# A two-layer hybrid encoder: ten of the sixteen gate tiles of each mixer's last two merges made in pairs by seven block products

## The chip, the cores and the metric

The kernel runs on one core of a Trainium2 chip, as one program that is launched once. The metric is the device time of that program in microseconds (us), the median of several executions. All data is f32; products are made on the matrix engine (TensorE, "PE" in the profile) from values split into a rounded high part and a low rest (`fp32r`). The other engines named here are VectorE (DVE), ScalarE (ACT), GpSimd (POOL) and the queue from which almost all transfers are issued (SP).

## The reference

Two layers work on x (512 tokens by 1024 features). Each is a half-step feed-forward net (FFN), a mixer, and a second FFN. What the change touches is the end of the mixer:

```python
proj = h @ w_in                                   # h: 512 x 1024
qa, ka, va, ub, qc, kc, vc, f_lin, g_lin = split(proj)
ya = chunked_relpos_attention(qa, ka, va)         # branch A
yb = multiscale_pool(ub)                          # branch B
yc = forgetting_attention(qc, kc, vc, f_lin)      # branch C
branch = einsum('bsnw,nwd->bsnd', [ya, yb, yc], w_branch)
gates = sigmoid(g_lin.reshape(B, S, 3, 1024))     # g_lin: 512 x 3072
merged = sum over the three branches of gates * branch
x = x + gate2 * (merged @ w_out)
```

So each branch needs a gate of 1024 features, a product of h with a 1024 x 1024 block of weights, and a product of its own output (512 wide) with 512 x 1024 weights.

## The kernel before

**Products.** Everything is kept transposed: features on the 128 partitions, the 512 tokens along the row. A weight chunk of 512 KB is loaded into a `raw` buffer (two exist), ACT casts it to the high part `whi`, DVE subtracts to get the low part `wlo` (three buffers each; `wchunk`, lines 262 to 280). `triple` (line 117) then issues three matmuls for each block of 128 features (high by high, high by low, low by high), each with 512 columns. The normed input h of a stage stands in `hhi` and `hlo`.

**A gate tile** (128 features of a gate for 512 tokens) is 8 such blocks, so 24 matmuls into one PSUM bank. The branch product of the same features is 4 blocks, 12 matmuls. `merge_units(l, n, ys, put)` (line 1053) walks the 8 tiles d of branch n: a chunk of `w_branch` for every second d, the gate's chunk, the gate's matmuls, a tanh on ACT, the branch's matmuls, and `put`, which multiplies the two (DVE), adds to the running sum `m` (POOL), and for the last branch splits the sum into high and low part (`put_b`, line 1138; in `v2` buffers for d below 4, else in `b` buffers).

**Order in the mixer** (`Mixer.run`): attention A, then attention C, with the merge of branch A filled in between its steps. Then the pooled branch's four `pool_front` (line 1010), each with a matmul group, sums over trailing windows on POOL, and a split of the result into a `ptb` buffer. Each is followed 60 units later by its `pool_back` (a unit is one matmul of 512 columns in the program's own count). In between run the merge of branch C (n = 2) and then that of branch B (n = 1). The product with `w_out` (`k_outer`) ends the mixer.

**The FFN's pairs.** In two of its three parts each FFN already makes two gate tiles together. `seven` (line 520) takes the two tiles' weights as a 2 x 2 block matrix (rows: the two tiles; columns: features 0 to 511 and 512 to 1023). The input is a 2 x 2 block matrix too (features by tokens, halves of each). It forms seven products of blocks in place of eight, each 4 blocks of 3 matmuls of 256 columns (`add_product`, lines 128 to 130). For that it needs sums of weight blocks (`tens`, line 529, into `v2`), split into `ptb` (two buffers), and sums of blocks of h, made ahead by `t_tasks` (lines 475 to 499) in `v2` or in place and split into eight `b` buffers. Partial results are copied (ACT) and added (DVE, 256 columns) in a `v2` buffer.

**Queues.** Each engine executes its instructions in the order of its queue. The order is set when the program is built: work is placed by program order and by when a planner expects its inputs. `later(delay, fn)` puts work off until the program's count of matmuls has advanced by `delay`; `poll` issues what is due. A buffer is given to a new tile when its last reader is done. There are 17 `b`, 4 `v2`, 4 `xv`, 3 `whi` and `wlo`, 2 `raw`, 2 `ptb` and 2 `t1` buffers in SBUF, and 4 `acc` and 4 `mm` banks in PSUM.

Of the kernel before, what the change touches and what calls it, by code (L numbers as in the profile page):

```python
# [15 lines left out]
F32 = mybir.dt.float32  # L16
F32R = mybir.dt.float32r
# [23 lines left out]
def encoder_kernel(tc, xT, c, w_ada, b_ada, gains, w_gate, w_up, w_down, w_qkv, w_f, w_ubg,  # L41
# [404 lines left out]

    class Ffn:
# [19 lines left out]

        def t_tasks(self):  # L470

            norm, bias = self.norm, modc[:, self.l, 3 * self.ms]
            self.tforms = [None] * 4
            first, second = slice(0, HALF), slice(HALF, T)
            sub = lambda o, a, b: nc.vector.tensor_tensor(o, a, b, op=ALU.subtract)
            full = [None] * 4

            def h(q):
                if norm is None:
                    full[q] = blk("v2", F32)  # L480
                    k = slice(2 * q, 2 * q + 2)
                    nc.vector.tensor_tensor(full[q], hhi[:, k, :].bitcast(F32), hlo[:, k, :].bitcast(F32), op=ALU.add)
                else:
                    full[q] = norm.xa[q]
                    for a in range(2):
                        d = 2 * q + a
                        nc.scalar.activation(full[q][:, a, :], full[q][:, a, :], AF.Identity, bias=bias[:, d:d + 1])

            def t1_t3(m):
                b1, b2 = full[m], full[m + 2]  # L490
                sub(b1[:, :, first], b1[:, :, second], b1[:, :, first])
                sub(b1[:, :, second], b2[:, :, second], b1[:, :, second])

            def t2_t4(m):
                b1, b2 = full[m], full[m + 2]
                sub(b2[:, :, second], b2[:, :, second], b1[:, :, first])
                sub(b2[:, :, first], b2[:, :, first], b2[:, :, second])

            def parts(q):
                self.tforms[q] = blk("b"), blk("b")  # L500
                split_to(*self.tforms[q], full[q])

            r = []
            for m in range(2):
                for fn, i in ((h, m), (h, m + 2), (t1_t3, m), (parts, m), (t2_t4, m), (parts, m + 2)):
                    r.append(lambda fn=fn, i=i: fn(i))
            return r

        def rights(self, name):

            first, second = slice(0, HALF), slice(HALF, T)
            if name[0] == "B":
                k0 = 4 * (int(name[1]) - 1)
                cols = (first, second)[int(name[2]) - 1]
                return [(hhi[:, k0 + k, cols], hlo[:, k0 + k, cols]) for k in range(4)]
            q0, cols = {"T1": (0, first), "T3": (0, second), "T4": (2, first), "T2": (2, second)}[name]
            tf = self.tforms
            return [tuple(part[:, k % 2, cols] for part in tf[q0 + k // 2]) for k in range(4)]

        def seven(self, which, n):  # L520

            src = (w_gate, w_up)[which][self.l, self.s]
            raws = []
            for i in range(2):
                side_work()
                raw = st([P, KD, P], F32, "raw", NRAW)
                last["dma"] = nc.sync.dma_start(raw, src[n + i]).ins
                raws.append(raw)
            tens = lambda o, a, b, op: nc.vector.tensor_tensor(o, a, b, op=op)
            a11, a12, a21, a22 = raws[0][:, :4], raws[0][:, 4:], raws[1][:, :4], raws[1][:, 4:]  # L530
            ah, al = st([P, KD, P], F32R, "whi", 3), st([P, KD, P], F32R, "wlo", 3)
            split_to(ah, al, raws[0])
            bh, bl = st([P, 4, P], F32R, "whi", 3), st([P, 4, P], F32R, "wlo", 3)
            split_to(bh, bl, a22)
            s12, s34 = st([P, 2, 4, P], F32, "v2", 4), st([P, 2, 4, P], F32, "v2", 4)
            tens(s12[:, 0], a21, a22, ALU.add)
            tens(s34[:, 0], a11, a21, ALU.subtract)
            tens(s12[:, 1], s12[:, 0], a11, ALU.subtract)
            tens(s34[:, 1], a12, s12[:, 1], ALU.subtract)
            sh, sl = st([P, 4, 4, P], F32R, "ptb", 2), st([P, 4, 4, P], F32R, "ptb", 2)  # L540
            split_to(sh[:, 0:2], sl[:, 0:2], s12)
            split_to(sh[:, 2:4], sl[:, 2:4], s34)
            lefts = {"A11": [(ah[:, k], al[:, k]) for k in range(4)],
                     "A12": [(ah[:, 4 + k], al[:, 4 + k]) for k in range(4)],
                     "A22": [(bh[:, k], bl[:, k]) for k in range(4)]}
            for i, name in enumerate(("S1", "S2", "S3", "S4")):
                lefts[name] = [(sh[:, i, k], sl[:, i, k]) for k in range(4)]
            x, y, w = acc((P, HALF)), acc((P, HALF)), acc((P, HALF))
            c = st([P, 4, HALF], F32, "v2", 4)
            go = lambda o, left, right, start: add_product(o, lefts[left], self.rights(right), start)  # L550
            go(x, "A11", "B11", True)
            nc.scalar.copy(c[:, 0], x)
            go(y, "A12", "B21", True)
            tens(c[:, 0], y, c[:, 0], ALU.add)
            go(x, "S2", "T2", False)
            nc.scalar.copy(c[:, 1], x)
            go(w, "S1", "T1", True)
            nc.scalar.copy(c[:, 2], w)
            go(x, "S3", "T3", False)
            nc.scalar.copy(c[:, 3], x)  # L560
            go(w, "S4", "B22", False)
            tens(c[:, 1], w, c[:, 1], ALU.add)
            tens(c[:, 3], c[:, 2], c[:, 3], ALU.add)
            go(x, "A22", "T4", False)
            return [[c[:, 0:2].rearrange("p a t -> p (a t)")], [x, c[:, 3]]]

        def silu(self, parts):
            sg = t1(T)
            n = T // len(parts)
            for i, p in enumerate(parts):  # L570
                nc.scalar.activation(sg[:, i * n:(i + 1) * n], p, AF.Silu)
            return sg

        def act(self, n, pg, pu, sg=None):
            if sg is None:
                sg = self.silu([pg])
            pr = t2(T)
            nc.vector.tensor_tensor(pr, pu, sg, op=ALU.mult)  # L578
            a = blk("b")
            split_to(a[:, 0, :], a[:, 1, :], pr)  # L580
            return a

        def run(self, nxt):
# [4 lines left out]
            for part, (f0, nf) in enumerate(parts):  # L588
                acts = []
                n = 0  # L590
                if part == 0 and self.norm is None:
                    acts = self.start()
                    n = 3
                    todo = self.t_tasks()
                elif part == 0:
# [18 lines left out]
                    todo = self.t_tasks()  # L614
                if part == 0:
                    for i in range(12):
                        later(T_FIRST + T_STEP * i, lambda i=i: todo.pop(0)() if len(todo) == 12 - i else None)
                elif part == 1:
                    while todo:
                        todo.pop(0)()  # L620
                MOD_RATE[0] = 0.5 if part else 1.0
                while part and n < nf:
                    both = [self.silu(p) for p in self.seven(0, f0 + n)]
# [386 lines left out]
    def pool_front(l, g):  # L1010
# [21 lines left out]
        b = st([P, 2, T], F32R, "ptb", 2)  # L1032
# [20 lines left out]
    def merge_units(l, n, ys, put):  # L1053
        wb = [None]
        gates = {}

        def gate_of(d):
            if d % 2 == 0:
                wb[0] = wchunk(w_branch[l, n, d:d + 2].rearrange("a p k c -> p a k c"), (2, 4, P))
            gh, gl = wchunk(w_ubg[l, 4 + n * KD + d], (KD, P))  # L1060
            pg = gates[d] = acc()
            for k in range(KD):
                triple(pg, gh[:, k, :], gl[:, k, :], hhi[:, k, :], hlo[:, k, :], k == 0, k == KD - 1)
                yield

        for d in range(KD):
# [6 lines left out]
            th = t1(T)  # L1073
            nc.scalar.activation(th, pg, AF.Tanh, scale=0.5)
# [13 lines left out]
    class Mixer:  # L1088
# [10 lines left out]
        def run(self, nxt):  # L1099
# [57 lines left out]
            mc = merge_units(l, 2, yc, put_c)  # L1157
# [5 lines left out]
            mb = merge_units(l, 1, yb, put_b)  # L1163
# [20 lines left out]
    FILL_A, FILL_C = 9.0, 9.0  # L1184

# [66 lines left out]
```

## Time and profile before

| what | value |
|---|---|
| time, median of 3 runs | 2426.74 us (2425.58 to 2429.62) |
| profiled execution | 2427.92 us, its span 2426.2 us |
| ACT busy | 1107.4 us |
| first mixer, pooled branch and last two merges | about 670 to 824 us of the span |
| second mixer, the same | about 1864 to 2024 us of the span |

The profile is of one execution. "Busy" is the time in which an engine had an instruction in work. Matmuls are pipelined, so the duration of one (about 0.39 us at 512 columns) is longer than the spacing from one start to the next. The spacing is what adds up. A page of grouped rows gives line, engine, operation, output and inputs, shape, count, busy us, mean ns of one, and the idle time just before with what ended it.

### The profile page before, as it was taken

How to read it: one execution, taken by the hardware profiler on the slowest of the kernel's cores; microseconds unless marked ns; L12 is line 12 of the kernel's file. 1: busy time of each engine (PE TensorE's matmuls, PEld its weight loads, DVE VectorE, ACT ScalarE, POOL GpSimd, SP SyncE). 2: the span in 40 equal slices, each digit the busy share in tenths (PEclk: the TensorE clock that was granted, in tenths of full speed). 3: DMA queues.
4: the chain of work that ended last, by engine and by line, in shares of the span. 5: the costliest groups of instructions: out<-in, count | busy, mean ns of one | idle time of the engine just before them, and what ended most of it. 6: DMA issues, size and time to landing. Idle time of an engine off the chain costs nothing. (4 is left out here: it accounts for less than half of the span.)

```text
span 2426.2 us, 33833 instructions
## 1 busy us (share of the span) xinstructions
PE 2386.2 (98%) x12954; PEld 2053.5 (85%) x12954; DVE 1555.2 (64%) x2750; ACT 1107.4 (46%) x1898; POOL 343.8 (14%) x423
## 2 busy tenths in 40 slices
PE   7999999999999999999999999999999999999999
PEld 5898988778788898989898989988788888889898
DVE  8977756787543378777468766477866434655463
ACT  5342444786532353424453424466765324534241
POOL 3000011144432210000000000112444222000000
PEclk9999999999999999999999999999999999999999
DMA  7746432223323326464326443323232233222232
GB/s 272 243 156 238 161 137 91 92 79 106 104 87 112 139 104 236 162 228 157 138 80 224 167 150 111 131 70 113 73 116 96 87 122 130 77 97 100 100 105 87
DMA packets 116278, 320.22 MB, mean 132 GB/s; under 512 B 11122, under 2 KB 13298, under 8 KB 116116
## 3 DMA queue, kind: packets, MB, share of 16 engines
q1 hardware_dynamic: 114962, 313.86, 37.5%
q0 software_dynamic: 1152, 4.19, 0.4%
q8 instruction: 102, 1.67, 0.3%
q14 instruction: 60, 0.49, 0.1%
q10 hardware_dynamic: 2, 0.00, 0.0%
HBM read 311.64 MB, written 6.38 MB: 131 GB/s over the span
## 5 line engine op out<-in xcount | busy, mean ns | idle before, releaser
L277 ACT CAST whi<-raw 128x1024 fp32r<-128x1024 f32 (+1 forms) x331 | 344.7, 1045 | 623.4 <-PE acc L120 284.1
L279 DVE TENSOR_TENSOR wlo<-raw,whi 128x1024 fp32r<-128x1024 f32 x323 | 398.2, 1235 | 277.1 <-ACT whi L277 273.3
L119 PE MATMUL acc<-b,whi 128*128 128x512 f32 (+1 forms) x960 | 360.5, 375 | 0.0
L121 PE MATMUL acc<-b,wlo 128*128 128x512 f32 (+1 forms) x960 | 356.7, 372 | 0.3 <-DVE wlo L279 0.3
L120 PE MATMUL acc<-b,whi 128*128 128x512 f32 (+1 forms) x960 | 356.9, 372 | 0.0
L119 PE MATMUL mm<-hhi,whi 128*128 128x512 f32 x792 | 309.1, 391 | 1.4 <-ACT whi L277 1.4
L120 PE MATMUL mm<-hlo,whi 128*128 128x512 f32 x792 | 308.6, 390 | 0.0
L121 PE MATMUL mm<-hhi,wlo 128*128 128x512 f32 x792 | 307.9, 389 | 0.0
L121 PEld LDWEIGHTS acc<-b,wlo 128*128 128x128 f32 x960 | 180.8, 188 | 32.2 <-DVE wlo L279 0.7
L119 PEld LDWEIGHTS acc<-b,whi 128*128 128x128 f32 x960 | 180.8, 188 | 31.5
L120 PEld LDWEIGHTS acc<-b,whi 128*128 128x128 f32 x960 | 180.9, 188 | 30.0
L206 DVE CUSTOM_DVE_ANT_0 v<-v,b,badac 128x1024 f32<-128x1024 f32 x144 | 188.0, 1316 | 20.3 <-DMA v<-in_w_ada_dram 19.9
L119 PE MATMUL acc<-hhi,whi 128*128 128x512 f32 x480 | 191.0, 399 | 3.9 <-ACT whi L277 2.2
L120 PE MATMUL acc<-hlo,whi 128*128 128x512 f32 x480 | 188.1, 392 | 1.1 <-DVE hlo L702 1.1
L121 PE MATMUL acc<-hhi,wlo 128*128 128x512 f32 x480 | 187.4, 391 | 0.0
L119 PEld LDWEIGHTS mm<-hhi,whi 128*128 128x128 f32 x792 | 149.1, 188 | 32.3 <-ACT whi L277 2.3
L121 PEld LDWEIGHTS mm<-hhi,wlo 128*128 128x128 f32 x792 | 148.7, 188 | 31.3
L120 PEld LDWEIGHTS mm<-hlo,whi 128*128 128x128 f32 x792 | 148.8, 188 | 29.3
L578 DVE TENSOR_TENSOR t<-mm,t 128x512 f32<-128x512 f32 x86 | 59.4, 691 | 139.7 <-PE mm L121 138.4
L119 PE MATMUL acc<-whi,hhi 128*128 128x512 f32 x336 | 137.8, 411 | 0.9 <-DVE xv L385 0.9
L121 PE MATMUL acc<-whi,hlo 128*128 128x512 f32 x336 | 132.0, 393 | 0.0
L120 PE MATMUL acc<-wlo,hhi 128*128 128x512 f32 x336 | 131.7, 392 | 0.0
(284 smaller groups left out, 5073.1 us busy)
## 6 DMA issues: line engine op xcount, KB each, us to landing
v<-in_w_ada_dram SPq DMA_DIRECT2D x144, 512.0 KB, 5.2
raw<-in_w_down_dram SPq DMA_DIRECT2D x88, 512.0 KB, 3.3
raw<-in_w_up_dram SPq DMA_DIRECT2D x82, 512.0 KB, 3.2
raw<-in_w_gate_dram SPq DMA_DIRECT2D x79, 512.0 KB, 3.2
raw<-in_w_ubg_dram SPq DMA_DIRECT2D x56, 512.0 KB, 3.2
raw<-in_w_qkv_dram SPq DMA_DIRECT2D x42, 512.0 KB, 3.7
raw<-in_w_branch_dram SPq DMA_DIRECT2D x24, 512.0 KB, 3.6
raw<-in_w_out_dram SPq DMA_DIRECT2D x16, 512.0 KB, 3.2
```

The lines of the kernel that those rows point to most:

```text
L119: mm(o, lh, rh, start=start, stop=False)
L120: mm(o, lh, rl, start=False, stop=False)
L121: mm(o, ll, rh, start=False, stop=stop)
L206: dot = nc.vector.tensor_tensor_reduce(out=raw, in0=raw, in1=silc[0], scale=1.0, scalar=badac[:, l, j, d:d + 1], op0=ALU.mult, op1=ALU.add ...
L277: nc.scalar.copy(hi, raw)
L279: lo_eng.tensor_tensor(lo, raw, hi.bitcast(F32), op=ALU.subtract)
L578: nc.vector.tensor_tensor(pr, pu, sg, op=ALU.mult)
```

## The change

`seven` and the block sums of h move out of the FFN class, unchanged in what they compute there, into a function `seven(srcs, blocks, bank)` and a class `Blocks`. In the mixer a `Blocks` is made after attention C, and its twelve steps are put off to 30, 45, ... 195 units. The merge of branch C makes tiles (4, 5) and (6, 7) by `seven`, that of branch B tiles (0, 1), (2, 3) and (4, 5), with their PSUM in the `mm` banks. The other six tiles stay as they are. In a paired tile the two gate chunks are loaded ahead of the branch chunk; before it was the other way round. `pool_front` splits into a `b` buffer in place of `ptb`; `put_b` always into `b`.

```diff
+    class Blocks:
+        def __init__(self, xa=None, bias=None):
+            self.xa, self.bias = xa, bias
+            self.full, self.parts = [None] * 4, [None] * 4
+            steps = ((self.h, 0), (self.h, 2), (self.t1_t3, 0), (self.split, 0), (self.t2_t4, 0), (self.split, 2))
+            self.todo = [lambda fn=fn, i=i + m: fn(i) for m in range(2) for fn, i in steps]
+        def schedule(self, start, step):
+            count = len(self.todo)
+            for i in range(count):
+                later(start + step * i, lambda i=i: self.todo.pop(0)() if len(self.todo) == count - i else None)
...
+        def h(self, q):
+            if self.xa is None:
+                self.full[q] = blk("v2", F32)
+                k = slice(2 * q, 2 * q + 2)
+                nc.vector.tensor_tensor(self.full[q], hhi[:, k, :].bitcast(F32), hlo[:, k, :].bitcast(F32), op=ALU.add)
...
+        def t1_t3(self, m):
+            b1, b2 = self.full[m], self.full[m + 2]
+            minus(b1[:, :, FIRST], b1[:, :, SECOND], b1[:, :, FIRST])
+            minus(b1[:, :, SECOND], b2[:, :, SECOND], b1[:, :, SECOND])
...
+        def split(self, q):
+            self.parts[q] = blk("b"), blk("b")
+            split_to(*self.parts[q], self.full[q])
...
+    def seven(srcs, blocks, bank):
...
+        ah, al = st([P, KD, P], F32R, "whi", 3), st([P, KD, P], F32R, "wlo", 3)
+        split_to(ah, al, raws[0])
+        bh, bl = st([P, 4, P], F32R, "whi", 3), st([P, 4, P], F32R, "wlo", 3)
+        split_to(bh, bl, a22)
+        s12, s34 = st([P, 2, 4, P], F32, "v2", 4), st([P, 2, 4, P], F32, "v2", 4)
+        tens(s12[:, 0], a21, a22, ALU.add)
+        minus(s34[:, 0], a11, a21)
+        minus(s12[:, 1], s12[:, 0], a11)
+        minus(s34[:, 1], a12, s12[:, 1])
+        sh, sl = st([P, 4, 4, P], F32R, "ptb", 2), st([P, 4, 4, P], F32R, "ptb", 2)
+        split_to(sh[:, 0:2], sl[:, 0:2], s12)
+        split_to(sh[:, 2:4], sl[:, 2:4], s34)
...
+        x, y, w = bank((P, HALF)), bank((P, HALF)), bank((P, HALF))
+        c = st([P, 4, HALF], F32, "v2", 4)
+        go(x, "A11", "B11", True)
+        nc.scalar.copy(c[:, 0], x)
+        go(y, "A12", "B21", True)
+        tens(c[:, 0], y, c[:, 0], ALU.add)
+        go(x, "S2", "T2", False)
+        nc.scalar.copy(c[:, 1], x)
+        go(w, "S1", "T1", True)
+        nc.scalar.copy(c[:, 2], w)
+        go(x, "S3", "T3", False)
+        nc.scalar.copy(c[:, 3], x)
+        go(w, "S4", "B22", False)
+        tens(c[:, 1], w, c[:, 1], ALU.add)
+        tens(c[:, 3], c[:, 2], c[:, 3], ALU.add)
+        go(x, "A22", "T4", False)
+        return [[c[:, 0:2].rearrange("p a t -> p (a t)")], [x, c[:, 3]]]
...
-        b = st([P, 2, T], F32R, "ptb", 2)
+        b = blk("b")
         split_to(b[:, 0, :], b[:, 1, :], df)
...
         def gate_of(d):
+            if d in paired:
+                blocks.finish()
+                both = seven([w_ubg[l, 4 + n * KD + d + i] for i in range(2)], blocks, mmt)
+                for i, p in enumerate(both):
+                    ths[d + i] = apply(p, AF.Tanh, scale=0.5)
+                    gates[d + i] = None
             if d % 2 == 0:
                 wb[0] = wchunk(w_branch[l, n, d:d + 2].rearrange("a p k c -> p a k c"), (2, 4, P))
+            if d in paired:
+                return
             gh, gl = wchunk(w_ubg[l, 4 + n * KD + d], (KD, P))
...
-                b = blk("v2" if d < 4 else "b")
+                b = blk("b")
...
-            mc = merge_units(l, 2, yc, put_c)
+            blocks = Blocks()
+            blocks.schedule(M_FIRST, M_STEP)
+            mc = merge_units(l, 2, yc, put_c, blocks, (4, 6))
...
-            mb = merge_units(l, 1, yb, put_b)
+            mb = merge_units(l, 1, yb, put_b, blocks, (0, 2, 4))
...
+    M_FIRST, M_STEP = 30, 15
```

More of the change, by code (lines that the diff above doesn't have):

```diff
@@ L447, in encoder_kernel, with apply @@
+    def apply(parts, func, **kw):
+        o = t1(T)
+        n = T // len(parts)
+        for i, p in enumerate(parts):
+            nc.scalar.activation(o[:, i * n:(i + 1) * n], p, func, **kw)
+        return o
     class Ffn:
@@ L465, in unit @@
                        k == 0, k == KD - 1)
[L470 to L572, printed above, removed]
         def act(self, n, pg, pu, sg=None):
             if sg is None:
-                sg = self.silu([pg])
+                sg = apply([pg], AF.Silu)
             pr = t2(T)
@@ L613, in run @@
                     n = 2
-                    todo = self.t_tasks()
+                    blocks = Blocks(self.norm.xa, modc[:, l, 3 * ms])
                 if part == 0:
-                    for i in range(12):
-                        later(T_FIRST + T_STEP * i, lambda i=i: todo.pop(0)() if len(todo) == 12 - i else None)
+                    blocks.schedule(T_FIRST, T_STEP)
                 elif part == 1:
-                    while todo:
-                        todo.pop(0)()
+                    blocks.finish()
                 MOD_RATE[0] = 0.5 if part else 1.0
                 while part and n < nf:
-                    both = [self.silu(p) for p in self.seven(0, f0 + n)]
+                    both = [apply(p, AF.Silu)
+                            for p in seven([w_gate[l, s, f0 + n + i] for i in range(2)], blocks, acc)]
                     for i, sg in enumerate(both):
@@ L1050, in wpool_load, with merge_units @@
         return w[:, 0], w[:, 1]
-    def merge_units(l, n, ys, put):
+    def merge_units(l, n, ys, put, blocks=None, paired=()):
         wb = [None]
-        gates = {}
+        gates, ths = {}, {}
         def gate_of(d):
+            if d in paired:
+                blocks.finish()
+                both = seven([w_ubg[l, 4 + n * KD + d + i] for i in range(2)], blocks, mmt)
+                for i, p in enumerate(both):
+                    ths[d + i] = apply(p, AF.Tanh, scale=0.5)
+                    gates[d + i] = None
             if d % 2 == 0:
                 wb[0] = wchunk(w_branch[l, n, d:d + 2].rearrange("a p k c -> p a k c"), (2, 4, P))
+            if d in paired:
+                return
             gh, gl = wchunk(w_ubg[l, 4 + n * KD + d], (KD, P))
@@ L1072, in merge_units @@
             bh, bl = wb[0]
[L1073 to L1074 removed]
+            th = ths[d] if d in ths else apply([pg], AF.Tanh, scale=0.5)
             pb = acc()
@@ L1156, in run @@
             wp = wpool_load(l)
-            mc = merge_units(l, 2, yc, put_c)
+            blocks = Blocks()
+            blocks.schedule(M_FIRST, M_STEP)
+            mc = merge_units(l, 2, yc, put_c, blocks, (4, 6))
             for gi in range(4):
```

37 lines of the change are left out of this document (36 added, 1 removed).

## The prediction

> **What bounds the kernel now.** I read the page's engine table first, then the stretches in which the edited code runs, then the matmuls one by one there and in the FFN, where the same seven products already run.
>
> ```profile
> PE 2386.2 (98%) x12954; PEld 2053.5 (85%) x12954; DVE 1555.2 (64%) x2750; ACT 1107.4 (46%) x1898; POOL 343.8 (14%) x423
> PEclk9999999999999999999999999999999999999999
> ```
>
> PE is busy for 98% of the span at the full granted clock. Busy can hide a slow pipeline, so the stretches of the second mixer come next; columns are the stretch, its length, and busy us (count) of PE, weight load, DVE, ACT and POOL, then clock, DMA share and GB/s.
>
> ```profile
> 1870.00:1900.00 30.00, 30.00 (x135) 24.79 (x135) 14.61 (x25) 12.38 (x19) 14.27 (x20) 1.00 0.23 79
> 1924.00:1956.00 32.00, 32.00 (x143) 26.50 (x142) 10.03 (x10) 8.15 (x10) 7.31 (x4) 1.00 0.28 99
> ```
>
> PE never rests in either. In the second (merge of branch C) DVE works 10 of 32 us, ACT 8. So a merge lasts as long as its matmuls take to stream, and DVE and ACT have room. The first row (the pooled branch) is tighter: DVE and POOL each work about half of it. The spacing of matmuls in a merge:
>
> ```profile
> 1940.20 0.39 PE L119 MATMUL acc<-hhi,whi 128*128 128x512 f32 x1
> ...
> 1945.64 0.39 PE L119 MATMUL acc<-b,whi 128*128 128x512 f32 x1
> ...
> 1948.36 0.39 PE L119 MATMUL acc<-hhi,whi 128*128 128x512 f32 x1
> ```
>
> A gate tile's 24 matmuls run from 1940.20 to 1945.64, 5.44 us (0.227 each); the branch's 12 take 2.72. In the FFN the 84 matmuls of one `seven` run from the first row below to the next product's start in the second:
>
> ```profile
> 316.28 0.28 PE L128 MATMUL acc<-hhi,whi 128*128 128x256 f32 x1
> ...
> 326.25 0.40 PE L119 MATMUL mm<-hhi,whi 128*128 128x512 f32 x1
> ```
>
> That is 9.97 us, 0.1187 each: more than half of 0.227, so part of what seven products save over eight is lost to the shorter rows.
>
> **The change, part by part: PE.** Five pairs in each mixer, ten in all. A pair's gates are 2 x 5.44 = 10.88 us before and 9.97 after, if `seven` runs here as it does there. That saves 0.91 us a pair, **9.1 us** in all. PE does not wait in this stretch, so the saving is on the path that sets the end.
>
> The Trainium skill ("TensorE: Matmul & The Clock Gate", Back-to-back issue gap) gives the spacing of a warm matmul as its columns over 2.4 GHz plus 2.5 ns: 215.8 ns at 512 columns, 109.2 at 256. By it, a pair would go from 10.36 to 9.17 us and ten would save 11.9. The rows above have 227 and 118.7, a fixed part some 10 ns larger, which weighs on 84 matmuls more than on 48; the sum goes by the rows.
>
> **DVE and ACT of a pair.** Durations of the same operations:
>
> ```profile
> L279 DVE TENSOR_TENSOR wlo<-raw,whi 128x1024 fp32r<-128x1024 f32 x323 | 398.2, 1235 | 277.1 <-ACT whi L277 273.3
> L529 DVE TENSOR_TENSOR v<-raw 128x512 f32<-128x512 f32 x32 | 22.0, 687 | 24.1 <-DMA raw<-in_w_gate_dram 24.1
> L385 DVE TENSOR_TENSOR ptb<-v,ptb 128x1024 fp32r<-128x1024 f32 x64 | 76.6, 1220 | 1.2 <-ACT ptb L384 1.2
> L529 DVE TENSOR_TENSOR v<-acc,v 128x256 f32<-128x256 f32 x64 | 27.1, 423 | 17.8 <-PE acc L130 17.7
> L384 ACT CAST ptb<-v 128x1024 fp32r<-128x1024 f32 x64 | 65.3, 1050 | 36.9 <-DVE v L529 36.8
> L552 ACT COPY v<-acc 128x256 f32<-128x256 f32 x32 | 11.9, 373 | 4.6 <-PE acc L130 3.6
> raw<-in_w_ubg_dram SPq DMA_DIRECT2D x56, 512.0 KB, 3.2
> ```
>
> DVE: the first chunk's low part 1.235, half of the second's 0.687 (taken as the 128x512 row), four sums of weights 4 x 0.687, two low parts of sums 2 x 1.220, three additions 3 x 0.423: 8.38 us, in place of 2 x 1.235. So 5.9 us more a pair. The time from one pair to the next is 9.97 + 2 x 2.72 = 15.4 us. DVE's other work in it is the branch chunk (1.235), two multiplications and, in the last merge, two splits (all near 0.69): 12.4 of 15.4 us. ACT adds two casts of 1.05 and four copies of 0.373, 3.6 us beyond what it casts now. Both fit, so I cost them at nothing; the cover is PE's own stream, and what it would cost without it is the rivals' matter. No transfer is added: the same chunks, 512 KB each, three in 15.4 us, each 3.2 us from issue to landing.
>
> **Does each pair get its operands in time?** A pair that follows a pair is the tight case. Take its predecessor's first product as time 0. The branch chunk of the pair before that one can be cast once a `whi` buffer is free; the row below shows a cast starting as the matmul L120 releases it.
>
> ```profile
> 1937.45 1.05 ACT L277 CAST whi<-raw 128x1024 fp32r<-128x1024 f32 x1 [6.61 <-PE acc L120]
> ```
>
> Cast and subtraction end at about 2.4, which frees a `raw` buffer for the second gate chunk: landed at 5.6. Four sums: 8.4. The `ptb` buffers come free with the sixth of seven products, at 8.55. Two casts and subtractions later (the second hides the first's) it is about 12. The first product that needs them is the third, at 15.4 + 2 x 1.42 = 18.3. Margin 6 us. The first chunk's own parts, which the pair's first two products need, come earlier (their `whi` buffer is free at 2.9; they are needed at 15.4).
>
> **The block sums of h**, once a mixer:
>
> ```profile
> L482 DVE TENSOR_TENSOR v<-hhi,hlo x4: 1215/1216/1227, 53.0 to 87.9; 128x1024 f32<-128x1024 f32 x4
> L475 DVE TENSOR_TENSOR v<-v,v x8: 681/686/692, 70.6 to 1249.3; 128x512 f32<-128x512 f32 x8
> ```
>
> DVE: 4 x 1.216 + 8 x 0.686 + 4 x 1.220 = 15.2 us; ACT 4 x 1.05. They are due from 30 to 195 units, 7 to 44 us after the pooled branch begins; the first pair begins after about 250 units, 57 us. The cover is PE's pooled and branch-C products. Within the row 1870 to 1900 above, DVE rises from 14.6 to about 25 of 30 us.
>
> That stretch has one chain with little room: the last `pool_front`, whose sums on POOL and split on DVE must be done when `pool_back` comes.
>
> ```profile
> 1895.84 1.28 POOL L1024 TENSOR_TENSOR strip<-strip 128x512 f32<-128x512 f32 x1
> 1898.74 0.69 DVE L385 TENSOR_TENSOR ptb<-ssum,ptb 128x512 fp32r<-128x512 f32 x1 [0.74 <-ACT ptb L384]
> 1902.76 0.40 PE L119 MATMUL acc<-ptb,pta 128*128 128x512 f32 x1
> ```
>
> Done at 1899.43, used at 1902.76: 3.3 us of room. POOL is also slowed when DVE works beside it:
>
> ```profile
> 1933.11 1.29 POOL L1134 TENSOR_TENSOR xv<-xv,t 128x512 f32<-128x512 f32 x1 [5.79 <-DVE t L1133]
> 1941.26 2.37 POOL L1134 TENSOR_TENSOR xv<-xv,t 128x512 f32<-128x512 f32 x1 [6.87 <-DVE t L1133]
> 1941.26 1.23 DVE L279 TENSOR_TENSOR wlo<-raw,whi 128x1024 fp32r<-128x1024 f32 x1
> ```
>
> The same addition takes 1.29 alone and 2.37 when a subtraction of 1.23 starts with it. The steps of `Blocks` come every 15 x 0.227 = 3.4 us and hold DVE for at most 2 x 0.69, so two of them can lengthen the chain on POOL and one can stand before its DVE part: 4.1 us at worst, 0.8 beyond the room. From both sides: 0 to 0.8 us a mixer.
>
> The Trainium skill ("SBUF — State Buffer", Who interferes with whom) has the reason: DVE with two SBUF inputs and GpSimd hold a shared port pair in turn, for a whole instruction. The 1.08 us between those two rows agrees, and by this rule the work added to DVE is felt by POOL as well.
>
> **First pair of a mixer.** Of the FFN's 32 `seven`, the page has 1.2 us of waiting in all, in front of product 5:
>
> ```profile
> L128 PE MATMUL acc<-b,ptb 128*128 128x256 f32 x384 | 107.9, 281 | 1.2 <-ACT v L556 1.2
> 130.81 1.05 ACT L277 CAST whi<-raw 128x1024 fp32r<-128x1024 f32 x1 [3.12 <-DMA raw<-in_w_up_dram]
> 131.76 0.37 ACT L556 COPY v<-acc 128x256 f32<-128x256 f32 x1
> ...
> 125.64 0.28 PE L128 MATMUL acc<-hhi,whi 128*128 128x256 f32 x1
> ...
> 136.57 0.40 PE L119 MATMUL mm<-hhi,whi 128*128 128x512 f32 x1
> ```
>
> There ACT stood 3.12 us at a cast whose chunk had not landed, with the copy that frees PE's accumulator queued behind it. That `seven`, the run's first, took 10.93 us (125.64 to 136.57), 0.96 longer. In a mixer I find no late chunk (the branch chunk's buffer, not its transfer, comes last), but I bound it at 0 to 1.0 us for the first pair.
>
> **Buffers moved.** `b` holds, before the first pair, 4 outputs of branch C, 4 of the pooled branch, 8 parts and in layer one a row of c: 17 of 17, none over. In the last merge branch C's four are free for the first splits and the eight parts for the rest. In the `w_out` product 8 splits, 4 blocks of the next norm, that row, and three prefetched chunks make 16. I take 0.
>
> **Sum.** -9.1, plus 0 to 2 x (0.8 + 1.0) = 3.6 of waits, of which I take 1.0, nearer to the FFN, whose 32 `seven` share 1.2 us: -8.1. The profiled execution took 2427.92 us, 1.2 above the median of the runs. 2427.92 - 8.1 - 1.2 = **2418.6 us**.
>
> **The rivals.**
>
> *ACT's queue, at every pair.* The copies of partial results stand behind a cast that waits for its chunk, as at 130.81. At 0.96 a pair this takes 9.6 and leaves +0.5: 2427.2. For it: a pair has only 5.4 us of other matmuls behind it here, against 10.9 in the FFN. Against it: the branch chunk's transfer can start when the weight sums are done and its cast needs a buffer that comes later still.
>
> *The weight sums come late: slower.* The place is the third product of each of the eight pairs that follow a pair. If DVE serves all its other work of a period first (12.4 less 5.2 of the chain, 7.2 us) and a chunk comes 3.1 us late, as it did at 130.81, the sums are ready at 12 + 7.2 + 3.1 = 22.3 and PE waits 4.0 us: 32 us over eight pairs. 2418.6 + 32 = **2450.6**. It decides against the change once the wait is 9.1/8 = 1.14 us a pair, at 19.4. For it: DVE would be 80% used and takes its queue in order. Against it: the margin of 6 us.
>
> *The pooled branch pays more*, 3 us a mixer, because its chain and the block sums of h push each other on both DVE and POOL: 2424. Against it: three of the twelve steps at most fall on the tight chain.
>
> *Weight loads in the open.*
>
> ```profile
> L130 PEld LDWEIGHTS acc<-b,ptb 128*128 128x128 f32 x384 | 72.3, 188 | 0.0
> ```
>
> 84 loads of 0.188 us are 15.8 us a pair if they did not overlap, 4.9 more than the 10.88 of now: 2427.9 - 1.2 + 49 = 2476. The FFN's 9.97 us for the same 84 speaks against it.
>
> **How the numbers follow.** What a measurement of this kernel can tell from no change is about 0.2%, 4.9 us. Forecast 0.72 (2416.5 to 2421.2: waits of 0 to 3.6, and a microsecond for the runs' own spread below); pooled branch 0.08; ACT's queue 0.10; late sums 0.09; loads 0.01. Faster: forecast and pooled branch less a part that falls short, 0.79. Same: 0.11. Slower: 0.10. Both signs do not share the chance evenly, so the range goes from 2416.0 over the pooled branch up to 2426.0, leaving late sums, loads and most of ACT's queue out. The forecast's own range is 2416.5 to 2421.2.
>
> **What would show each step.** Right: ten runs of 84 matmuls of 256 columns in the mixers, 9.97 us from first to next product; 15.4 us from pair to pair in the last merge; DVE about 90 us busier (ten pairs of 5.9 and two times 15.2); PE still without waits after the pooled branch. Wrong: waits of PE ended by a copy on ACT (rival one), by a low part in `ptb` on DVE (rival two), or before `pool_back`'s three matmuls (rival three). The prediction fails if those waits come to more than 5 us, or if `seven` takes longer than 9.97 without any.

## The result, and the profile after

The changed kernel takes **2445.16 us** (median of 6 runs, 2442.43 to 2447.21), beside 2426.71 for the kernel before (6 runs, 2425.58 to 2429.62). The ratio is 1.0073, 95% interval 1.0063 to 1.0083. So it became slower by 0.7%; 2418.6 had been predicted, in a range up to 2426.0. The profiled execution took 2444.26 us, its span 2442.5, which is 16.3 more than the span before.

The engine table of the changed kernel, and the same kind of stretches as before (the pooled branch of the second mixer in two pieces, then the merge with pairs; columns as in the prediction):

```profile
PE 2385.4 (98%) x13314; PEld 2066.8 (85%) x13314; DVE 1649.4 (68%) x2872; ACT 1143.0 (47%) x1976; POOL 343.9 (14%) x423
```

```profile
1877.00:1907.00 30.00, 28.91 (x130) 23.65 (x130) 25.50 (x32) 10.62 (x16) 14.80 (x19) 1.00 0.20 62
1907.00:1921.00 14.00, 7.73 (x26) 5.86 (x25) 5.81 (x9) 4.22 (x7) 3.67 (x5) 0.76 0.20 75
1935.00:1967.00 32.00, 32.00 (x223) 29.91 (x222) 23.33 (x30) 15.09 (x23) 6.26 (x4) 1.00 0.31 99
```

DVE is 94 us busier, as forecast, and the pairs (last row) run with PE full. But in the pooled branch (first two rows) DVE works 25.5 of 30 us, and then PE works only 7.7 of 14 us, at a granted clock of 0.76. The 98% of the page hides that.

**The pairs give what was forecast.** First matmul of a pair in the mixer, and the first one behind it:

```profile
1941.32 0.28 PE L128 MATMUL mm<-hhi,whi 128*128 128x256 f32 x1
...
1951.29 0.40 PE L119 MATMUL acc<-b,whi 128*128 128x512 f32 x1
```

9.97 us, against 10.88 for two gate tiles. Six of the ten pairs take this; the other four, the last two of each mixer's last merge, take 11.29, 10.83, 12.45 and 10.83: 5.5 us in all.

**The loss is in the pooled branch.** From the last matmul of attention C's last weighted sum to the fourth `pool_back` (called *the stretch* below) the kernel before takes 32.51 and 32.54 us in the two mixers, the changed one 43.12 and 42.38: 20.45 more. Its ends in the second mixer, before (the other end, 1902.76, stands in the prediction) and after:

```profile
1870.22 0.28 PE L980 MATMUL mm<-ptb,v 128*128 128x128 f32 x1
```

```profile
1877.67 0.28 PE L987 MATMUL mm<-ptb,v 128*128 128x128 f32 x1
...
1920.05 0.39 PE L119 MATMUL acc<-b,pta 128*128 128x512 f32 x1
```

With -9.1 and +5.5 that makes +16.85. The spans differ by 16.3, but that the two are so near is partly luck: up to the stretch of mixer one both kernels issue the same 3434 matmuls, and there the changed kernel's profiled execution happens to be 2.2 us shorter (671.14 against 673.33). From there to its end it is 18.5 us longer, as the medians are (18.45). So about 1.7 us of the loss have no place in this account.

PE's waits in the changed kernel by who ended them (total, times, longest):

```profile
PE acc L119 <- DVE b L1049: 12.5, 2, 6.3
...
PE acc L121 <- DVE wlo L279: 3.4, 3, 1.3
PE mm L128 <- ACT v L542: 3.4, 4, 1.2
```

The first row is new. L1049 is the DVE half of `pool_back`'s evacuation, which frees an `acc` bank. PE stands like this once in each mixer, here in the second:

```profile
1907.26 0.39 PE L121 MATMUL acc<-b,wlo 128*128 128x512 f32 x1
1913.91 0.80 PE L119 MATMUL acc<-hhi,whi 128*128 128x512 f32 x1 [6.27 <-DVE b L1049]
1914.50 0.63 PE L120 MATMUL acc<-hlo,whi 128*128 128x512 f32 x1
1914.93 0.63 PE L121 MATMUL acc<-hhi,wlo 128*128 128x512 f32 x1
```

Two losses show: 6.65 us from the start of one matmul to the start of the next (waits of PE are given so below, where 0.23 is usual), and then matmuls spaced 0.43 us apart where 0.227 is usual. Twelve spacings of 0.427 and one of 0.59 follow in mixer one (2.8 us over the usual), eight and one in mixer two (2.0). Why was the bank late? ACT's queue over that time:

```profile
1901.11 0.62 ACT L384 CAST b<-ssum 128x512 fp32r<-128x512 f32 x1 [6.68 <-DVE ssum L1038]
1901.64 1.05 ACT L384 CAST b<-v 128x1024 fp32r<-128x1024 f32 x1
1902.59 0.68 ACT L1048 ACTIVATE b<-acc,psc 128x512 fp32r<-128x512 f32 x1
...
1910.37 0.62 ACT L384 CAST b<-ssum 128x512 fp32r<-128x512 f32 x1 [5.67 <-DVE ssum L1038]
1910.89 1.04 ACT L384 CAST b<-v 128x1024 fp32r<-128x1024 f32 x1
1911.84 0.68 ACT L1048 ACTIVATE b<-acc,psc 128x512 fp32r<-128x512 f32 x1
```

and in the kernel before (where these lines are L384 and L1041):

```profile
1886.52 0.69 ACT L1041 ACTIVATE b<-acc,psc 128x512 fp32r<-128x512 f32 x1 [1.74 <-PE acc L121]
1889.70 0.62 ACT L384 CAST ptb<-ssum 128x512 fp32r<-128x512 f32 x1 [2.50 <-DVE ssum L1031]
```

Before, `pool_back` 0 is evacuated (1886.52) ahead of the third `pool_front`'s split (1889.70): with two `ptb` buffers that split has to wait until `pool_back` 0 is done with its own. After, the split has one of 17 `b` buffers, so it is queued ahead of the evacuation. ACT stands 6.68 us in front of it, because the windowed sums that it splits are not ready, with the finished product behind it. At 1910.37 the fourth split holds up the second evacuation in the same way.

And why were the windowed sums not ready? DVE in that stretch, grouped, and POOL's windowed additions over the whole run:

```profile
L452 DVE TENSOR_TENSOR v<-v,v 128x512 f32<-128x512 f32 x4 | 5.2, 1294 | 0.0
L477 DVE TENSOR_TENSOR v<-hhi,hlo 128x1024 f32<-128x1024 f32 x4 | 4.8, 1219 | 0.6 <-PE mm L987 0.6
L279 DVE TENSOR_TENSOR wlo<-raw,whi 128x1024 fp32r<-128x1024 f32 x3 | 4.5, 1497 | 0.0
L452 DVE TENSOR_TENSOR v<-v 128x512 f32<-128x512 f32 x4 | 2.8, 688 | 0.1
```

```profile
L1031 POOL TENSOR_TENSOR strip<-strip 128x512 f32<-128x512 f32 x12 | 16.9, 1412 | 0.5
```

```profile
L1024 POOL TENSOR_TENSOR strip<-strip 128x512 f32<-128x512 f32 x12 | 13.0, 1081 | 0.5
```

The first fence is the window 1877 to 1901: all twelve additions and subtractions of the block sums of h (four of L477, eight of L452) run in these 24 us, in the middle of the four windowed sums. POOL's addition of two strips takes 1412 ns on average in the changed kernel (second fence) where it took 1081 before (third), and DVE's own operations are stretched too (L452 with two inputs 1294 ns against 0.69 us, the low part of a weight chunk 1497 against 1235). Each side slows the other. How much of the delay is DVE's own queue and how much POOL's slower additions, no run separates.

**The four long pairs.** ACT, POOL and PE in the fourth pair of the second mixer, the second of its last merge:

```profile
1989.56 0.62 ACT L384 CAST b<-xv 128x512 fp32r<-128x512 f32 x1 [3.26 <-POOL xv L1149]
1990.09 1.04 ACT L277 CAST whi<-raw 128x1024 fp32r<-128x1024 f32 x1
1991.03 0.36 ACT L538 COPY v<-mm 128x256 f32<-128x256 f32 x1
```

```profile
1988.23 1.29 POOL L1149 TENSOR_TENSOR xv<-xv,t 128x512 f32<-128x512 f32 x1 [13.71 <-DVE t L1148]
```

```profile
1991.45 0.39 PE L128 MATMUL mm<-b,ptb 128*128 128x256 f32 x1 [0.78 <-ACT v L538]
```

`put_b` adds on POOL (L1149) and then splits. ACT stands 3.26 us at that split's cast, and the copy of the pair's first partial result (L538), which PE's third product needs, comes after it.

### The profile page after: what moved, and what is told of

It is laid out like the page before. It is cut to its first block, busy times and chain, and to the rows that moved or that the text cites. A ratio compares the mean times of both kernels' runs of the same rounds, so it can differ in the third digit from the quotient of the medians.

```text
span 2442.5 us, 34766 instructions
## 1 busy us (share of the span) xinstructions
PE 2385.4 (98%) x13314; PEld 2066.8 (85%) x13314; DVE 1649.4 (68%) x2872; ACT 1143.0 (47%) x1976; POOL 343.9 (14%) x423
## 5 line engine op out<-in xcount | busy, mean ns | idle before, releaser
L277 ACT CAST whi<-raw 128x1024 fp32r<-128x1024 f32 (+1 forms) x311 | 323.6, 1044 | 530.9 <-PE acc L120 175.8
L279 DVE TENSOR_TENSOR wlo<-raw,whi 128x1024 fp32r<-128x1024 f32 x303 | 380.4, 1258 | 187.4 <-ACT whi L277 184.5
L119 PE MATMUL acc<-b,whi 128*128 128x512 f32 (+1 forms) x1024 | 382.4, 373 | 0.0
L121 PE MATMUL acc<-b,wlo 128*128 128x512 f32 (+1 forms) x1024 | 378.2, 369 | 1.3 <-DVE wlo L279 1.3
L120 PE MATMUL acc<-b,whi 128*128 128x512 f32 (+1 forms) x1024 | 378.6, 370 | 0.0
L121 PEld LDWEIGHTS acc<-b,wlo 128*128 128x128 f32 x1024 | 193.0, 188 | 34.5 <-DVE wlo L279 1.7
L119 PEld LDWEIGHTS acc<-b,whi 128*128 128x128 f32 x1024 | 193.0, 188 | 32.7 <-DVE xv L434 0.3
L120 PEld LDWEIGHTS acc<-b,whi 128*128 128x128 f32 x1024 | 193.1, 189 | 30.9
L119 PE MATMUL acc<-hhi,whi 128*128 128x512 f32 x320 | 131.1, 412 | 16.4 <-DVE b L1049 12.5
L121 PE MATMUL acc<-hhi,wlo 128*128 128x512 f32 x320 | 127.9, 401 | 2.2 <-DVE wlo L279 2.2
L120 PE MATMUL acc<-hlo,whi 128*128 128x512 f32 x320 | 128.0, 400 | 0.4 <-DVE hlo L709 0.4
```

The lines of the kernel that those rows point to most:

```text
L119: mm(o, lh, rh, start=start, stop=False)
L120: mm(o, lh, rl, start=False, stop=False)
L121: mm(o, ll, rh, start=False, stop=stop)
L277: nc.scalar.copy(hi, raw)
L279: lo_eng.tensor_tensor(lo, raw, hi.bitcast(F32), op=ALU.subtract)
```

## The experiments

All ratios are against the kernel before, run beside them. *Stretch* is as above, for mixer one and two.

| run | median us | ratio, 95% interval | stretch, us |
|---|---|---|---|
| sums_alone | 2444.95 | 1.0076 [1.0060, 1.0093] | 42.78, 41.81 |
| buffers_alone | 2429.52 | 1.0011 [1.0002, 1.0021] | 34.51, 34.56 |
| ptb_back | 2431.70 | 1.0026 [1.0015, 1.0037] | 36.20, 35.59 |
| py_in_mm | 2436.81 | 1.0042 [1.0027, 1.0057] | 33.90, 33.90 |
| sums_late | 2442.33 | 1.0059 [1.0043, 1.0074] | 41.36, 41.04 |
| add_on_dve | 2442.24 | 1.0061 [1.0047, 1.0074] | 43.11, 43.10 |
| ptb_late_dve | 2426.05 | 0.9993 [0.9985, 1.0002] | 34.48, 34.20 |
| ptb_mm_dve | 2428.75 | 1.0003 [0.9995, 1.0012] | 34.77, 34.77 |
| pairs_only | 2420.48 | 0.9976 [0.9966, 0.9985] | 32.54, 32.54 |
| sums_held | 2434.07 | 1.0032 [1.0019, 1.0044] | 32.54, 32.54 |
| sums_held_b | 2432.81 | 1.0026 [1.0016, 1.0036] | 36.19, 34.62 |
| four_pairs_spread | 2422.26 | 0.9981 [0.9972, 0.9990] | 32.51, 32.54 |

### Pairs, sums or buffers?

**sums_alone**: the changed kernel without its pairs; the block sums are made and not read.

```diff
-            mc = merge_units(l, 2, yc, put_c, blocks, (4, 6))
+            mc = merge_units(l, 2, yc, put_c)
...
-            mb = merge_units(l, 1, yb, put_b, blocks, (0, 2, 4))
+            mb = merge_units(l, 1, yb, put_b)
```

> No pairs: all sixteen gate tiles by eight blocks as before; block sums of h made at 30 to 195 units but unread, buffers moved as in the change. If the two long waits before a gate's first matmul (6.6 us each, then 13 matmuls at 0.43 us) come from what is done in the pooled branch and not from the pairs, they stay: 2427 + 2 x (6.4 + 2.9 + 1.2) = about 2448. If the pairs cause them: about 2427.

All of the loss is there without a single pair, with the same waits of 6.65 us. The changed kernel's pairs save 9.1 and lose 5.5 us, and yet it is no faster than this one: the stretches, 0.9 us shorter here, and the 1.7 us without a place above make up most of that difference. **buffers_alone** takes the block sums away too (`blocks = None`), so that only the moved buffers are left:

> Only the buffers moved (pool_front's split and put_b's always in b); no sums, no pairs. Theory A, the long wait is the sums' work on DVE and POOL's slowing: no wait, 2427. Theory B, the long wait is that a free b buffer lets ACT's queue take the split of the third pool_front ahead of the evacuation of the first pool_back, which then holds its PSUM bank: part of the wait appears without any sums, 2430 to 2440.

The moved buffers alone cost 2 us a mixer, and the time, 2429.52, ends just below the range of theory B. ACT's order is already the bad one:

```profile
1887.60 0.62 ACT L384 CAST b<-ssum 128x512 fp32r<-128x512 f32 x1 [4.87 <-DVE ssum L1038]
1888.12 0.68 ACT L1048 ACTIVATE b<-acc,psc 128x512 fp32r<-128x512 f32 x1
...
1896.49 0.62 ACT L384 CAST b<-ssum 128x512 fp32r<-128x512 f32 x1 [6.27 <-DVE ssum L1038]
1897.02 0.68 ACT L1048 ACTIVATE b<-acc,psc 128x512 fp32r<-128x512 f32 x1
```

The evacuations stand behind the splits here as well, but without the block sums the fourth split comes 28.2 us after the start of the stretch (1868.25); in the changed kernel it came 32.7 us after it (1877.67). PE waits only 2.1 us, once in each mixer, before a gate. **ptb_back** is the other corner, the changed kernel with `pool_front`'s split in `ptb` again:

```diff
-        b = blk("b")
+        b = st([P, 2, T], F32R, "ptb", 2)
```

> The changed kernel with pool_front's split back in ptb, everything else as changed (sums at 30 to 195 units, ten pairs). Theory B: ACT evacuates the first pool_back ahead of the third split again, the bank comes free in time, the two long waits shrink below 1.5 us each and the clock stays up: 2445 - 2 x (6 + 2.6) = about 2428 or less. Theory A: the waits stay above 4 us, 2440 or more.

Block sums and pairs with the old buffers make the stretch 3.7 and 3.1 us longer than before, with no standstill of 6 us and the clock at 1.00. The longest wait left there is 1.9 us, and the time, 2431.70, lies between the two theories' bounds: theory B names what makes the long waits, but the sums cost something without it. So the moved buffer costs 2.0 a mixer alone, the sums about 3.4, and both together about 10. That is more than their sum: with the sums, PE's wait for the second evacuation grows from 2.1 to 6.65 us, and then the clock falls as well (2.8 and 2.0 of the 10).

**py_in_mm**: `pool_back` takes its bank from `mm` in place of `acc` (`py = mmt()`), so that its late evacuation blocks no gate tile.

> The changed kernel with pool_back's product in an mm bank (free in this stage) in place of an acc bank; the queues of ACT and DVE are as in the changed kernel. If what PE waits for is the bank that the late evacuation holds, the 6.6 us waits before the gate go, and what is left is the wait of the fourth pool_back for its split (it is done 4.4 us after PE stands at the gate, and PE gets there 5.4 us later): 0 to 2 us each; 2445 - 2 x (5 + 2.6) = about 2430. If it is the operands that are late, nothing changes: 2445.

The 6.65 us are gone, as they must be if it was the bank. But the time, 2436.81, lies between the 2430 and the 2445 expected: part of the loss moved instead of going. Waits of 1.3 and 2.0 us come up some 9 us later in the gate tiles, with slow matmuls behind them in mixer one.

### Can the sums be put elsewhere?

**sums_late**: due times moved (`M_FIRST, M_STEP = 130, 10`).

> The changed kernel with the twelve steps of the block sums due at 130 to 240 units in place of 30 to 195, so after the pooled sums on POOL; buffers as changed (b). If the sums in the pooled stretch are the larger part (sums and moved buffers alone cost 10 us a mixer, moved buffers alone 2): the 6.6 us wait falls to about 2 us and no slow clock follows; 2445 - 2 x 8 = about 2429. If the order of ACT's queue alone decides: it stays above 2438.

A clear miss: 2442.33. DVE's rows say why:

```profile
1895.39 2.13 DVE L452 TENSOR_TENSOR v<-v,v 128x512 f32<-128x512 f32 x2
1897.45 2.06 DVE L279 TENSOR_TENSOR wlo<-raw,whi 128x1024 fp32r<-128x1024 f32 x1
1899.43 1.52 DVE L452 TENSOR_TENSOR v<-v 128x512 f32<-128x512 f32 x1
```

The sums are still there, before the third split (1901.74). The first of the twelve additions and subtractions starts 0.3 us ahead of the stretch, as in the changed kernel, and the last ends, counted from there, within 0.2 us of where it did; only the splits came later. A due time only says when the instruction is handed to the planner. The planner then put it where its inputs were ready, and h has long been ready.

**sums_held**: the sums held for certain, by an edge in DVE's queue behind the fourth split (with `ptb`, the addition of **add_on_dve**, below, and due times of 130 to 240 units). `after("pool")` issues an instruction behind `last["pool"]` on its engine; `split[0]` is the DVE half of `pool_front`'s split.

```diff
+                        with after("pool"):
+                            self.todo.pop(0)()
...
                 b = pool_front(l, gi)
+                last["pool"] = split[0]
```

> Whole computation; pool_front's split in ptb, put_b's addition on DVE, and each step of the block sums held by an edge in DVE's queue behind the fourth pool_front's split, so that none stands in the pooled stretch (due times alone did not do that: the planner takes the sums forward). Theory: pooled stretch 32.5 to 33 us, sums done in the 22 us between the fourth pool_back and the first pair, 2418 to 2422. Rival (the sums cost about the same wherever they lie, since DVE must also make the gates' low parts and the first pair's weight sums there): the stretch is short, but the gate tiles and the first pair wait for wlo or for the parts of the sums, 2424 to 2429.

The stretch is back at 32.54, to the digit. And the time is 2434.07: the rival was right, beyond its own price. DVE and PE right after the fourth split:

```profile
1907.83 2.32 DVE L279 TENSOR_TENSOR wlo<-raw,whi 128x1024 fp32r<-128x1024 f32 x1
...
1912.41 1.21 DVE L483 TENSOR_TENSOR v<-hhi,hlo 128x1024 f32<-128x1024 f32 x1
1913.55 0.74 DVE L1055 SCALAR_TENSOR_TENSOR b<-acc,psc,b 128x512 fp32r<-128x512 f32 x1
1914.21 1.21 DVE L387 TENSOR_TENSOR b<-v,b 128x1024 fp32r<-128x1024 f32 x1
1915.34 1.21 DVE L279 TENSOR_TENSOR wlo<-raw,whi 128x1024 fp32r<-128x1024 f32 x1
```

```profile
1911.75 0.39 PE L119 MATMUL acc<-b,whi 128*128 128x512 f32 x1
1916.61 0.79 PE L121 MATMUL acc<-hhi,wlo 128*128 128x512 f32 x1 [4.47 <-DVE wlo L279]
```

DVE has no idle time; the low part of a gate chunk stands behind the sums (L483 and L387 are lines of `h` and of the split here), and PE stands for 4.9 us, in mixer one for 4.2. The clock falls here too: matmuls 0.43 us apart behind these waits cost another 1.6 and 3.0 us. 15.2 us of sums, and the weight sums of the first pair, do not fit into the 21 us before that pair (in **pairs_only**, below) together with the gates' own work. **sums_held_b**, the same with the split in `b`:

> As sums_held, but with pool_front's split in b as in the changed kernel. Theory (the moved buffer alone costs about 2 us a mixer as in buffers_alone, and costs 7 to 10 only together with sums in the pooled stretch): stretch 34.5 us, about 4 us over sums_held. Rival (the order on ACT with b is bad by itself once pairs are there): stretch 40 us or more, 2432 or more.

The stretch comes out near the theory (36.19, of which 1.7 is slow clock, and 34.62), so the moved buffer costs about 2 us here too, and the rival's 40 falls. The time is not the 4 us above sums_held that the theory gave but 1.3 below: PE's idle times before a gate's low part are shorter (2.8 us at most against 4.5).

### The pairs themselves

**add_on_dve**: `put_b`'s addition on DVE in place of POOL (`put_c(d, pb, th, nc.vector)`), all else as changed.

> The changed kernel with the last merge's running sum added on DVE in place of POOL. Theory: the 5.5 us that the pairs of the last merge wait come from put_b's cast, which waits for POOL on ACT's queue ahead of a pair's copies. Then the second and third pair of the last merge take 9.97 to 10.5 us in place of 10.8 to 12.5, and the time falls by 4 to 5: about 2440. The rival, that the pairs wait for their weight sums or a chunk: the pairs stay above 10.8 and the time at 2445.

Nine of the ten pairs now take 9.97 us, one 10.35: the cause of the long pairs was the cast that waits for POOL. Of the 5.5 us 5.1 are gone from the pairs, while the stretch in mixer two is 0.7 longer. Beside the kernel before, the loss falls by 3.9 us, from 18.45 to 14.55; 2442.24 stays above the 2440 expected.

**pairs_only**: the pairs without the block sums (the products with T1 to T4 take blocks of h itself, so the paired gates are not the right ones), with `ptb` and the addition on DVE.

> Leaves out the block sums of h: the products with T1 to T4 take the blocks of h themselves; pool_front's split is in ptb as before, put_b's addition is on DVE. Theory (the pairs are worth their 9.1 us; the loss is the block sums in the pooled stretch, the order on ACT that the moved buffer lets in, and put_b's cast in front of the pairs' copies): all ten sevens 9.97 us, 32.5 to 33 us from the last weigh matmul to the fourth pool_back, 2417.5 to 2420. Rival (the pairs cost something of their own, in the weights or the queues around them): 2424 or more, with waits in the merges.

Nine pairs at 9.97 us and one at 10.33, the stretch at 32.54, no wait of note in the merges. The rows add up to a gain of 8.7 us; the median gained 6.1 (0.9966 to 0.9985, so 3.6 to 8.3 us) and ends half a microsecond above the bound given. So the pairs' gain is real, though not all of it shows in the median, and the 15.2 us of block sums are what cannot be hidden where they are.

**ptb_late_dve** (`ptb`, sums due from 110 in steps of 12, addition on DVE) and **ptb_mm_dve** (`ptb`, `pool_back` in `mm`, addition on DVE) put the remedies together:

> Pairs as changed; pool_front's split back in ptb, block sums due at 110 to 242 units, last merge's addition on DVE. If these three causes are all, the pairs' own saving of 9.1 us is left with 1 to 4 us of waits: 2419 to 2422, below the kernel before. If pairs cost something besides, 2425 or more.

> As the last, but the sums at 30 to 195 units as in the change, and pool_back's product in an mm bank. From the run with ptb alone (2431.7, 3.1 to 3.7 us lost a mixer in the pooled stretch) the addition takes 4 to 5 off and the bank the 0.5 to 1.3 us waits before the gate: 2424 to 2427.

Both end where the kernel before is, and both miss what was expected (2419 to 2422, and 2424 to 2427). The stretch is still 1.7 to 2.3 us longer than before. From there to the first pair ptb_late_dve takes 0.8 us and ptb_mm_dve 1.9 us more than pairs_only, with a wait for the low part of a gate chunk in each. In ptb_mm_dve all ten pairs take 9.97 us.

**four_pairs_spread**: one pair of branch C's merge given back, so that the first pair comes 16 us later, and the sums spread over that time, each behind the latest weight chunk's low part.

```diff
-            mc = merge_units(l, 2, yc, put_c, blocks, (4, 6))
+            mc = merge_units(l, 2, yc, put_c, blocks, (6,))
...
-    M_FIRST, M_STEP = 30, 15
+    M_FIRST, M_STEP = 150, 14
...
+                        with after("pool"), after("wlo"):
```

> Whole computation. Four pairs a mixer instead of five (tile pair 4 of the merge of branch C goes back to two gate tiles), so the first pair comes 16 us later; pool_front's split in ptb, put_b's addition on DVE; each step of the block sums is held in DVE's queue behind the fourth pool_front's split and behind the low part of the latest weight chunk, due from 150 to 304 units. Theory (the sums need a place on DVE in which no low part of a gate chunk stands behind them; a window of 38 us instead of 22 gives it): stretch 32.5 us, no wait over 1 us in the merges, eight sevens of 9.97 us, 2426.5 - 8 x 0.91 = 2419.2, 2418 to 2422. Rival (the sums cost PE time wherever they lie in a mixer, since the planner puts several of them in one place): waits for wlo before a gate tile of branch C as in sums_held, 2425 or more.

The time is 2422.26: 4.2 us faster than the kernel before (0.9981, 0.9972 to 0.9990), and 0.3 above the range given. Its two stretches in the second mixer, the pooled one and from there to the first pair:

```profile
1866.50:1899.20 32.70, 32.70 (x147) 27.02 (x146) 17.59 (x27) 13.12 (x20) 14.23 (x20) 1.00 0.22 74
1899.00:1936.70 37.70, 37.70 (x168) 31.16 (x166) 31.84 (x34) 15.88 (x19) 8.14 (x5) 1.00 0.27 94
```

PE is full in both. DVE works 31.8 of 37.7 us in the second: that is where the sums now are, and it is nearly all the room there is. Beside sums_held it has both more room and the edge behind the low parts; no run separates the two.

## Why the prediction was wrong

Step by step, as the prediction put it:

- **-9.1 us from ten pairs: right where it is made.** A pair takes 9.97 us where nothing holds it up: nine of ten when the addition is moved (the tenth 10.35), ten of ten in ptb_mm_dve. In the medians less of it shows (see the end of this section).
- **The weight sums of consecutive pairs, margin 6 us: right.** No wait of PE for their parts shows. The slow rival of the prediction (2450.6) has nearly the measured time, but that is a coincidence: its place is not where the time went.
- **DVE about 90 us busier: right** (94).
- **"The block sums of h": covered by PE's products, 0 to 0.8 us a mixer: wrong, and the largest share.** The load was foreseen: about 25 of 30 us of DVE, measured 25.5. Its cost was not: ptb_back puts them at about 3.4 a mixer with the old buffers; on top of the moved ones (buffers_alone to sums_alone) they cost 8.3 and 7.3. Two things failed in the step. It took the due times (7 to 44 us) as the times of execution, one step in 3.4 us, at most three in the tight chain; all twelve additions and subtractions ran within 24 us (the four splits behind them), and later due times did not move them. And it asked only whether the last `pool_front` still meets its `pool_back`, and counted DVE's idle time over 30 us as cover. That time had owners: the low parts of gate chunks and the chain through POOL, both stretched by contention.
- **"Buffers moved ... I take 0": wrong.** The step counted whether `b` has room for all its tiles, and no wait shows that it lacks any. What it did not ask is what the old shortage did: two `ptb` buffers kept the split behind the evacuation on ACT. buffers_alone prices that at 2 us a mixer, and together with the sums it is what takes the loss from 3.4 to 10.
- **"DVE and ACT of a pair ... I cost them at nothing": wrong by 5.5 us** for the pairs in which `put_b` splits into the same queue. The sum of busy times (both fit in 15.4 us) was right and beside the point: one cast that waits 3.26 us for POOL holds all copies behind it. The rival "ACT's queue, at every pair" named the victim, the copies, but another cause, a chunk that lands late. No chunk did.
- The rival "the pooled branch pays more" named the place and the mutual slowing of DVE and POOL, at 3 us a mixer and a chance of 0.08. With the old buffers its size is about right (ptb_back: 3.7 and 3.1). But the sign it gave, waits before `pool_back`'s own matmuls, does not show in the changed kernel: PE stands before a gate, for a bank. That part came with the moved buffer, which the rival did not have, and with it the cost is 10.

The fall in clock (2.8 and 2.0 us) was not foreseen at all.

Left open: how much of the pairs' saving reaches the median. pairs_only gains 6.1 us of 8.7, four_pairs_spread 4.2 of 7.1. Their profiled spans gain more (8.6 and 7.0), but one span settles little. In the profiles here the stretch of mixer one begins anywhere from 669.8 to 674.7 us, after the same 3434 matmuls. The profiled execution before also lies 1.4 to 1.5 us above the medians of the kernel before beside these two runs, and their own lie 1.1 and 1.2 below theirs. From that point on, the profile of four_pairs_spread gains 7.2 us, as its pairs should, and that of pairs_only 6.5. The 2.2 us that pairs_only lacks lie ahead of mixer two's stretch: from there on it gains 4.1, where its pairs should give 4.2.

## What to carry to other kernels

Work that is "covered by idle time" needs a place in a queue: list what stands behind it on its engine, and who waits for that; a due time in program order is no place if a planner may take the work forward. A buffer pool that is short also orders instructions, so giving it more room can put an instruction that waits ahead of one that is ready. And a gain on the matrix engine is only worth what its preparation on the vector engine leaves: four pairs with room for the sums (four_pairs_spread, 4.2 us faster than before) beat five without it (sums_held, 7.5 slower).

## What the runs showed of the hardware

In these runs a standstill of PE could cost more than its length. After the 6.65 us the granted clock was 0.50, with matmuls of 512 columns 0.427 us apart:

```profile
1913.90:1918.00 4.10, 4.09 (x10) 3.23 (x11) 2.34 (x3) 0.63 (x2) 1.27 (x1) 0.50 0.35 128
```

The Trainium skill ("TensorE: Matmul & The Clock Gate", Part 1: The HAM clock gate) says that after an idle window of about 3.4 us the array runs at half its clock until it has been busy for such a window, with 426.7 ns between matmuls of 512 columns; by the 0.427 us and 0.50 above, the trace agrees. In sums_held_b a wait of only 2.15 us, 1.76 of it idle, had the same effect once and not the other time; in mixer one (first row) seven matmuls were 0.427 apart, in mixer two (second row) none:

```profile
701.80:707.00 5.20, 5.12 (x15) 4.05 (x16) 5.20 (x8) 1.25 (x3) 0.97 (x1) 0.67 0.00 0
1901.60:1907.00 5.40, 5.32 (x23) 4.38 (x24) 5.40 (x8) 1.42 (x4) 1.17 (x1) 1.00 0.00 0
```

So a wait shorter than that window can bring the low clock too. DVE and POOL slow each other by up to about the length of one instruction of the other: a low part of 1.21 us took 2.06 and 2.32 beside a POOL addition, and POOL's addition of two strips, 1.04 at best, took 1.90 beside a low part.
